# The second MLP products of a two-layer encoder: half of the features by seven block products in place of eight

## The chip, the cores and the metric

The kernel runs on one core of a Trainium2 chip. The metric is the device time of one execution, in microseconds (us). A core has five engines with instruction queues of their own, each worked through in order: TensorE (PE in the profile, its weight loads PEld) multiplies matrices and writes to PSUM, VectorE (DVE) and ScalarE (ACT) do elementwise work on SBUF and PSUM, GpSimd (POOL) elementwise work on SBUF, and SyncE (SP) starts the DMAs from HBM. Semaphores hold an instruction back until what it needs is there.

## The reference

A trunk of two layers on 256 tokens of width 1024, in float32. Each layer has an attention mixer, different in the two layers, and a squared-ReLU MLP with 4096 hidden features. Only the MLP is touched here:

```python
def rms_norm(x, g):
    xf = x.astype(jnp.float32)
    y = xf * lax.rsqrt(jnp.mean(xf * xf, axis=-1, keepdims=True) + RMS_EPS)
    return (y * g.astype(jnp.float32)).astype(x.dtype)

def sq_relu_mlp(xn, w1, w2):
    return jnp.square(jax.nn.relu(xn @ w1)) @ w2

for layer in range(DEPTH):
    ...
    x = x + sq_relu_mlp(rms_norm(x, norm_mlp[layer]), mlp_w1[layer], mlp_w2[layer])
return rms_norm(x, norm_final)
```

The second product is (256 tokens x 4096) times (4096 x 1024) in each layer.

## The kernel before, in words

All weights arrive from HBM in chunks of 128 x 2048 float32 (1 MB). TensorE multiplies in fp32r, a rounded float32, so each operand is split in two: a high half (the value rounded to fp32r, a cast by ScalarE, L227) and a low half (what the rounding left, a subtraction by VectorE, L228). A product a·b is then three matmuls, high·high, high·low, low·high, which `mm3` (L230 to L233) adds up in one PSUM bank. In the up product of the MLP the first two are one matmul of 512 columns, since the high and low halves of x lie side by side (L417), and the third is one of 256 (L420).

The MLP takes 16 blocks of 256 hidden features. For block j, `up(j)` computes the hidden features of all 256 tokens from chunk w1[j] in two PSUM banks; ScalarE copies the part from x's low half to SBUF (`side`, L423), VectorE adds it (`u`, L424) and makes relu(u) times u (`hsq`, L426), and the result is split into `hh` and `hl`. It lies as hidden features x tokens: two blocks of 128 features (f), each with 256 tokens. The second product of block j takes chunk w2[j]: for both f, both blocks of 128 tokens (t) and both halves of the 1024 output features there is one `mm3` with 128 stationary token columns and 512 moving weight columns: 8 `mm3`, 24 matmuls of 512 columns. They add up in four banks, `acc`, over the 16 blocks. The second products run three blocks behind the up products, so a step of the loop holds the second product of j and the up product of j + 3. The last two (first MLP) or three (second MLP) chunks are kept for the end and worked off bank by bank, so that what follows can begin with the first bank.

The order of the work: `weight()` (L218) hands out chunks in the order of `specs`, in which w1 and w2 chunks alternate; on each call it starts the DMA of the chunk four ahead and has the split of the chunks up to two ahead written down. There are four raw buffers and three pairs of split ones, so the split of a chunk waits until PE is done with the one three before it. A scheduler then sets the order of each engine's queue by the order in the program and by priorities, and sets the waits.

GpSimd has next to no work: a few constants, four copies, two memsets and five small powers. `y` (in `hand_over_tokens`) takes the four banks of the first MLP, scaled by each token's inverse norm, to the transposes that make x feature-first again; `finish` adds the second MLP to x, norms it and writes it out.

Of the kernel before, what the change touches and what calls it, by code (L numbers as in the profile page):

```python
# [76 lines left out]
def trunk(ctx, tc, a, out):  # L77
# [29 lines left out]
    def quarter_pair(name):  # L107
        return [act.tile([P, KT // 2, T], F32R, tag="quarter", name=name + v, bufs=4) for v in "hl"]

    def bank(tag):  # L110
        return ps.tile([P, 512], F32, tag=tag, name=tag)

# [31 lines left out]
    specs = []  # L144

    def plan(name, n):
# [25 lines left out]

    parts = {}
# [12 lines left out]

    def split_tiles(j):

        z = [wsp.tile([P, WCH + P], F32R, tag=n, name=n) for n in ("whi", "wlo")]
        return [z[0][:, specs[j][2][0]:specs[j][2][0] + WCH + (LINE if specs[j][3] else 0)], z[1][:, specs[j][2][1]:specs[j][2][1] + WCH]]  # L190

# [8 lines left out]
    def split_piece(eng=None):  # L200
        j, i = divmod(state["split"], WPARTS)
        if i == 0:
            parts[j][1:] = split_tiles(j)
        raw, hi, lo = (z[:, cut(j, i, WPARTS)] for z in parts[j])
        state["split"] += 1
        if specs[j][3] and i == WPARTS - 1:
# [133 lines left out]
    def hand_over_tokens(accs, last, n, scale):  # L340
# [4 lines left out]
        def leave(h, t):  # L345
            last(h, t)
            acc, sc = accs[2 * t + h], column(scale, t)
            with tc.high_priority(NORM_PRIO):
                y = ys[h, t] = scratch([512], "y")
                nc.scalar.activation(y[:, 0:T], acc[:, 0:T], AF.Copy, scale=sc)  # L350
                nc.vector.tensor_scalar(y[:, T:2 * T], acc[:, T:2 * T], sc, None, ALU.mult)
# [47 lines left out]

    def mlp(mp, xT, s, invert, tail, make_down, beside=lambda j: None):  # L400


        hs = {}

        def up(j):
# [3 lines left out]

            pu = [bank("w") for _ in range(2)]  # L410

# [14 lines left out]
            nc.vector.scalar_tensor_tensor(h, u, 0.0, u, ALU.max, ALU.mult)  # L426
# [7 lines left out]
        inv = invert()  # L434
        accs = open_accs()
        down = make_down(accs, hs)
# [7 lines left out]
        return accs, hs, inv, {j: weight() for j in tail}  # L444

# [7 lines left out]
    def mlp_between(mp, xT, s):  # L453
        def down(accs, hs):
            def step(j, w, f):
                for i in range(4):
                    down_tokens(accs[i], hs, j, w, f, i // 2, i % 2 * 512, i % 2 * 512 + 512, (j, f) == (0, 0), False)
            return step

        accs, hs, inv, w = mlp(mp, xT, s, lambda: inverse_columns(s), range(14, 16), down)  # L460

        def last(h, t):
            for j in w:
                for f in range(2):
                    down_tokens(accs[2 * t + h], hs, j, w[j], f, t, h * 512, h * 512 + 512, False, (j, f) == (15, 1))

        return accs, last, inv

    def finish(mp, xT, s):
# [3 lines left out]
        xt = mp.tile([P, NT, D], F32, name="xt")  # L473
        tail = range(13, 16)

        mm = down_tokens

        def down(accs, hs):
            def step(j, w, f):
                for i in range(4):  # L480
                    end = tail[0] - 1 if i == 3 else 15
                    mm(accs[i], hs, j, w, f, i // 2, (i % 2) * 512, (i % 2) * 512 + 512, (j, f) == (0, 0), (j, f) == (end, 1))
            return step

        def tokens_first(j):

            if j % 2 == 0 and j < 8:
                t, h = j // 4, j // 2 % 2
                pt = bank("w")
# [4 lines left out]
        accs, hs, inv, w = mlp(mp, xT, s, lambda: inverse_columns(s), tail, down, tokens_first)  # L494
        jf = [(j, f) for j in w for f in range(2)]
        for j, f in jf:
            for h in range(2):
                mm(accs[h], hs, j, w[j], f, 0, h * 512, h * 512 + 512, False, (j, f) == (15, 1))

# [3 lines left out]
        def square_sum(v, o):  # L503
            nc.scalar.activation(scratch([v.shape[-1]], "junk"), v, AF.Square, scale=D ** -0.5, accum_out=o)

        ss = small.tile([P, 4], F32, tag="ssf", name="ss")
        for h, cs in enumerate(HALF):
# [10 lines left out]
        ss = small.tile([P, 4], F32, tag="ssf", name="ss")  # L518
        xg = mp.tile([P, D], F32, name="xg")
        residual(1, HALF[1], accs[3])  # L520
        for i, (c0, c1) in enumerate(((0, 512), (512, 768), (768, D))):
            acc = bank("w") if i else accs[2]
            for n, (j, f) in enumerate(jf):
# [631 lines left out]
def _layout(i):  # L1155
# [25 lines left out]
    d["w1"] = f(i["mlp_w1"].reshape(2, KT, P, 16, 256).transpose(0, 3, 2, 1, 4).reshape(2, 16, P, WCH))  # L1181
    d["w2"] = f(i["mlp_w2"].reshape(2, 16, 2, P, D).transpose(0, 1, 3, 2, 4).reshape(2, 16, P, WCH))

# [31 lines left out]
```

## Time and profile before

| what | value |
|---|---|
| median of three runs | 736.88 us (736.64 to 737.38) |
| profiled execution, its own time | 737.34 us |
| span of the profile | 735.5 us |
| granted PE clock | 0.998 |
| busy: PE, DVE, ACT, POOL | 727.9, 544.2, 473.5, 8.3 us |
| moved from HBM | 127.16 MB read, 174 GB/s over the span |

The span is the time from the first to the last instruction; what lies around it is 1.84 us here. In a row of a group of instructions stand the line of the program, engine, operation, output and inputs by name with their shapes, the count, then after the bar the time in which any of them ran, the mean duration of one in ns, and the idle time before them with what ended it. In a row of the timeline stand the start, the duration, and the same names. Matmuls overlap in the records: one of 512 columns lasts some 390 ns but the next starts after 227, so a step is counted by starts. The first MLP's products run from 113 to 290 us, the second's from 551 to 729 us.

### The profile page before, as it was taken

The page shows a single profiled execution, that of the slowest core. Times are in us where ns is not written, and L with a number is a line of the kernel's source. Part 1 is how long each engine was busy: PE and PEld are TensorE (multiplying, and loading weights), DVE is VectorE, ACT ScalarE, POOL GpSimd, SP SyncE. Part 2 cuts the span into 40 slices and gives each one's busy share as a digit, 9 for nine tenths or more (in the row PEclk, how much of TensorE's full clock was granted, in tenths as well). Part 3 has the DMA queues.
Part 4 walks back from the last instruction along what each step waited for, and adds up shares of the span by engine and source line. Part 5 has one row for each costly group of instructions (what it writes and reads, how often), then busy time and mean ns, then how long its engine had stood idle before and what let it go on. Part 6 is the DMA issues. An engine that isn't in the chain of part 4 may idle for free.

```text
span 735.5 us, 12087 instructions
## 1 busy us (share of the span) xinstructions
PE 727.9 (99%) x4539; PEld 628.8 (85%) x4539; DVE 544.2 (74%) x1159; ACT 473.5 (64%) x1073; POOL 8.3 (1%) x20
## 2 busy tenths in 40 slices
PE   9999999999999999999999999999999999999996
PEld 7988998888888887888888888888898888888885
DVE  6788859766665666789978886899559765665674
ACT  6788967554455456577877668696857555455441
POOL 0100000000000001000000000000000000000000
PEclk9999999999999999999999999999999999999999
DMA  9873335564555554645664554455545555555501
GB/s 285 323 261 113 115 115 172 179 223 172 194 206 176 204 192 155 230 160 182 206 221 144 191 181 175 147 194 186 178 153 187 214 172 196 203 174 188 211 3 57
DMA packets 24730, 133.17 MB, mean 181 GB/s; under 512 B 3680, under 2 KB 5088, under 8 KB 10336
## 3 DMA queue, kind: packets, MB, share of 16 engines
q1 hardware_dynamic: 24528, 132.28, 52.2%
q8 instruction: 35, 0.57, 0.3%
q14 instruction: 23, 0.19, 0.1%
q10 hardware_dynamic: 144, 0.13, 0.1%
HBM read 127.16 MB, written 1.05 MB: 174 GB/s over the span
## 4 chain that ended last, share of the span: by engine, by line
PE 93%; ACT 2%; DVE 1%; issue 1%; DMA 1%; SPq 0%; POOLq 0%; POOL 0%; DVEq 0%
PE w L417 16%; PE acc L231 13%; PE acc L232 13%; PE acc L233 13%; PE acc L932 10%; PE w L420 8%; PE acc L937 5%; PE acc L584 3%; PE w L1044 1%; PE w L240 1%; PE w L231 1%; PE w L795 1%; PE w L232 1%; PE w L233 1%; PE w L809 1%
## 5 line engine op out<-in xcount | busy, mean ns | idle before, releaser
L228 DVE TENSOR_TENSOR wlo<-raw,whi 128x512 fp32r<-128x512 f32 (+3 forms) x527 | 307.5, 625 | 67.0 <-ACT whi L227 66.1
L227 ACT CAST whi<-raw 128x512 fp32r<-128x512 f32 (+3 forms) x527 | 269.2, 570 | 134.9 <-PE acc L233 57.0
L417 PE MATMUL w<-pair,whi 128*128 128x512 f32 x512 | 122.3, 391 | 0.0
L417 PEld LDWEIGHTS w<-pair,whi 128*128 128x128 f32 x512 | 95.5, 188 | 20.0 <-DVE pair L268 0.5
L231 PE MATMUL acc<-whi,hh 128*128 128x512 f32 x250 | 98.1, 392 | 0.0
L232 PE MATMUL acc<-wlo,hh 128*128 128x512 f32 x250 | 97.8, 391 | 0.0
L233 PE MATMUL acc<-whi,hl 128*128 128x512 f32 x250 | 97.6, 390 | 0.0
L932 PE MATMUL acc<-pair,whi 128*128 128x512 f32 x384 | 96.5, 398 | 0.0
L932 PEld LDWEIGHTS acc<-pair,whi 128*128 128x128 f32 x384 | 69.4, 188 | 13.7 <-issue 0.2
L420 PEld LDWEIGHTS w<-pair,wlo 128*128 128x128 f32 x512 | 63.0, 188 | 2.7
L424 DVE TENSOR_TENSOR u<-w,side 128x256 f32<-128x256 f32 x64 | 27.0, 422 | 51.4 <-ACT side L423 51.3
L420 PE MATMUL w<-pair,wlo 128*128 128x256 f32 x512 | 63.5, 277 | 0.0
L227 ACT CAST hh<-hsq 128x512 fp32r<-128x512 f32 x32 | 19.9, 622 | 56.6 <-DVE hsq L426 56.6
L233 PEld LDWEIGHTS acc<-whi,hl 128*128 128x128 f32 x250 | 47.0, 188 | 9.8
L231 PEld LDWEIGHTS acc<-whi,hh 128*128 128x128 f32 x250 | 47.0, 188 | 8.9
L232 PEld LDWEIGHTS acc<-wlo,hh 128*128 128x128 f32 x250 | 46.9, 188 | 8.8
L937 PEld LDWEIGHTS acc<-pair,wlo 128*128 128x128 f32 x384 | 47.7, 188 | 2.1
L937 PE MATMUL acc<-pair,wlo 128*128 128x256 f32 x384 | 49.0, 278 | 0.0
L231 PE MATMUL acc<-whi,pair 128*128 128x512 f32 x80 | 32.2, 403 | 0.0
L232 PE MATMUL acc<-wlo,pair 128*128 128x512 f32 x80 | 31.3, 391 | 0.0
L233 PE MATMUL acc<-whi,pair 128*128 128x512 f32 x80 | 31.2, 390 | 0.0
L1035 ACT ACTIVATE pp<-sn,dmn 128x384 f32<-128x384 f32 x32 | 19.6, 613 | 9.0 <-DVE dmn L1033 8.2
(221 smaller groups left out, 1103.0 us busy)
## 6 DMA issues: line engine op xcount, KB each, us to landing
raw<-in_w SPq DMA_DIRECT2D x64, 1024.0 KB, 4.8
raw<-in_w_oqk SPq DMA_DIRECT2D x24, 1024.0 KB, 4.9
raw<-in_w_ov SPq DMA_DIRECT2D x12, 1024.0 KB, 4.9
raw<-in_w_qk SPq DMA_DIRECT2D x4, 1024.0 KB, 9.3
raw<-in_w_oe SPq DMA_DIRECT2D x4, 1024.0 KB, 5.2
sw<-qk SPq DMA_DIRECT2D x64, 64.0 KB, 2.0
raw<-in_w_oo SPq DMA_DIRECT2D x4, 1024.0 KB, 5.6
bias<-in_rpb SPq DMA_DIRECT2D x8, 256.0 KB, 3.8
```

The lines of the kernel that those rows point to most:

```text
L227: a = nc.scalar.copy(hi, src).ins
L228: return a, (eng or nc.vector).tensor_tensor(lo, src, hi.bitcast(F32), op=ALU.subtract).ins
L231: nc.tensor.matmul(o, sh, mh, start=first, stop=False)
L232: nc.tensor.matmul(o, sh, ml, start=False, stop=False)
L233: nc.tensor.matmul(o, sl, mh, start=False, stop=last)
L417: nc.tensor.matmul(two(pu[f]), w[0][:, late(cut_of(k, f)) if (k, f) == (KT - 1, 1) else cut_of(k, f)], xT[2][:, k], start=k == 0, stop=False)
L420: nc.tensor.matmul(pu[f][:, 0:T], w[1][:, cut_of(k, f)], xT[0][:, k, :], start=False, stop=k == KT - 1)
L424: nc.vector.tensor_tensor(u[:, f], pu[f][:, 0:T], side[:, f], op=ALU.add)
L584: nc.tensor.matmul(o[:, 0:n], xs[i], (w[1], w[1], w[2])[i], start=(k, i) == (0, 0), stop=(k, i) == (KT - 1, 2))
L932: nc.tensor.matmul(two(hold["p"][f]), hold["w"][0][:, late(c) if f == 1 and k == KT - 1 else c], xp[:, k], start=k == 0, stop=False)
L937: nc.tensor.matmul(hold["p"][f][:, 0:T], hold["w"][1][:, c], xh[:, k, :], start=False, stop=k == KT - 1)
L1035: nc.scalar.activation(pp, sn, AF.Exp, bias=mn, scale=-1.0, accum_out=z)
```

## The change

The second products are done in another way for the first 14 blocks of the first MLP and the first 13 of the second (`SEVEN`).

One half of the output features (512) is computed as before, with two banks (`sums`, one for each token block). For the other half, hidden features x tokens is seen as 2 x 2 blocks of 128 x 128 (f and t), and the weights as 2 x 2 blocks of 128 x 256. A 2 x 2 block product by Strassen's method (in Winograd's form) needs seven products in place of eight. Each is one `mm3` with 256 moving columns, 21 matmuls of 256 columns, which add up over the blocks j in seven half banks (`seven_at`). The method needs four sums of token blocks and four sums of weight blocks for each j. GpSimd makes them: `wsum` (1024 columns, three instructions, written down where the chunk's DMA is) and `hsum` (512 columns, four instructions of 128, after `hsq`). The sums are split like everything else, into `uh`, `ul` and the second half of `whi`, `wlo`; three of the four weight blocks themselves are needed as well and go to `sh`, `sl`. Behind the loop the seven sums are put together to the 2 x 2 result (`second`) by a copy and four additions, and added in `hand_over_tokens` and `finish`.

The banks for this come from the up product: PSUM's second group of four is now `w1` and `w2` with two banks each; from the fourth up product on it has only the two of `w1`. The buffers of `hh` and `hl` go from four to three.

```diff
+SEVEN = (14, 13)
...
     def bank(tag):
-        return ps.tile([P, 512], F32, tag=tag, name=tag)
+
+        if tag == "w":
+            tag, turns[0] = ("w1", "w1", "w2", "w2")[turns[0] % 4], turns[0] + 1
+        return ps.tile([P, 512], F32, tag=tag, name=tag, bufs=4 if tag == "acc" else 2)
...
+            if j - 2 < SEVEN[layer]:
+                seven.add(len(specs))
             specs.append((a["w2"][layer, j - 2], WCH, (0, 0), False))
...
         parts[j] = [raw, None, None]
+        if j in seven:
+
+            r, v = raw[:, 1024:WCH], state["mp"].tile([P, 1024], F32, tag="wsum", name="wsum", bufs=3)
+            nc.gpsimd.tensor_tensor(v[:, 0:512], r[:, 256:768], r[:, 0:512], op=ALU.subtract)
+            nc.gpsimd.tensor_tensor(v[:, 512:768], r[:, 512:768], v[:, 0:256], op=ALU.subtract)
+            nc.gpsimd.tensor_tensor(v[:, 768:1024], v[:, 512:768], r[:, 768:1024], op=ALU.subtract)
+            sums[j] = v
...
         state["split"] += 1
+        if j in seven:
+            raw, *z = parts[j]
+            for y, c, src in (((z[0:2], (0, 1024), raw[:, 0:1024]),), (), ((z[4:6], (0, T), raw[:, 1024:1280]), (z[4:6], (T, 3 * T), raw[:, 1536:WCH])),
+                              ((z[2:4], (0, 1024), sums[j]),))[i]:
+                split(*(v[:, slice(*c)] for v in y), src, eng)
+            return
...
-            hs[j] = tuple(mp.tile([P, 512], F32R, tag=n, name=n, bufs=4) for n in ("hh", "hl"))
+            hs[j] = tuple(mp.tile([P, 512], F32R, tag=n, name=n, bufs=3) for n in ("hh", "hl"))
             split(*hs[j], h)
+            if j < tail[0]:
+
+                q, v = [h[:, tok(i)] for i in range(4)], mp.tile([P, 4, P], F32, tag="hsum", name="hsum", bufs=2)
+                for o, x0, x1, op in ((0, q[1], q[3], ALU.add), (1, q[0], q[1], ALU.subtract), (2, q[3], v[:, 1], ALU.subtract),
+                                      (3, q[2], v[:, 2], ALU.subtract)):
+                    nc.gpsimd.tensor_tensor(v[:, o], x0, x1, op=op)
+                hs[j] += tuple(mp.tile([P, 512], F32R, tag=n, name=n, bufs=3) for n in ("uh", "ul"))
+                split(*hs[j][2:], v.rearrange("p a b -> p (a b)"))
...
         for j in range(tail[0]):
             w = weight()
+            for b, half, (of, at), c in products:
+                o, l, m = seven_at[b][:, half * T:half * T + T], [z[:, tok(at)] for z in hs[j][2 * of:2 * of + 2]], [z[:, c % 4 * T:c % 4 * T + T] for z in w[2 + c // 4 * 2:][:2]]
+                mm3(o, *l, *m, j == 0 and half == 0, j == tail[0] - 1 and (half == 1 or b == 3))
             for f in range(2):
-                down(j, w, f)
+                for t in range(NT):
+                    down_tokens(sums[t], hs, j, w, f, t, f * -512, f * -512 + 512, (j, f) == (0, 0), False)
+            beside(j)
             if j + 3 < 16:
                 up(j + 3)
-            beside(j)
...
+        z, g = scratch([2, T], "z"), mp.tile([P, 4, T], F32, name="second")
+        nc.scalar.copy(z, two(seven_at[2]))
+        side = lambda v: v.unsqueeze(1).broadcast_to([P, 2, T])
+        nc.vector.tensor_tensor(g[:, 0:4:3], two(seven_at[0]), side(z[:, 0]), op=ALU.add)
+        nc.vector.tensor_tensor(g[:, 1:3], two(seven_at[1]), side(g[:, 3]), op=ALU.add)
+        nc.vector.tensor_tensor(g[:, 1:4:2], g[:, 1:3], side(z[:, 1]), op=ALU.add)
+        nc.vector.tensor_tensor(g[:, 2], g[:, 2], seven_at[3][:, 0:T], op=ALU.subtract)
```

GpSimd's queue in the first MLP. Before, between the last copy of the first mixer and the first memset of the second:

```order
L742 COPY ktok<-kpe 128x4x32 [waits DVE_49,PE_49]
L871 MEMSET k_0_3291 128x1024 [waits DVE_49,PE_49]
```

With the change, one step of the loop and the start of the next stand there (`raw` is a weight chunk, `wsum` and `hsum` the sums):

```order
L199 TENSOR_TENSOR wsum<-raw 128x512 [waits DMAHW7_49,Activation_49]
L200 TENSOR_TENSOR wsum<-raw,wsum 128x256 [waits Pool_49]
L201 TENSOR_TENSOR wsum<-wsum,raw 128x256 [waits Pool_49]
L474 TENSOR_TENSOR hsum<-hsq 128x128 [waits DVE_49,Activation_49]
L474 TENSOR_TENSOR hsum<-hsq 128x128
L474 TENSOR_TENSOR hsum<-hsq,hsum 128x128 [waits Pool_49] x2
L199 TENSOR_TENSOR wsum<-raw 128x512 [waits DMAHW1_49,Activation_49]
```

Seven instructions of 1536 columns a step are new, and the sums of a step's tokens stand ahead of those of a later chunk's weights.

VectorE's queue for one step in the middle of the first MLP, before (`whi`, `wlo` are the halves of a weight chunk, `w` a bank of the up product):

```order
L228 TENSOR_TENSOR wlo<-raw,whi 128x512 [waits DMAHW4_49,Activation_49]
L228 TENSOR_TENSOR wlo<-raw,whi 128x512 [waits Activation_49] x2
L228 TENSOR_TENSOR wlo<-raw,whi 128x384 [waits Activation_49]
L228 TENSOR_TENSOR wlo<-raw,whi 128x128 [waits Activation_49]
L424 TENSOR_TENSOR u<-w,side 128x256 [waits Activation_49]
L228 TENSOR_TENSOR wlo<-raw,whi 128x512 [waits DMAHW5_49,PE_49]
L228 TENSOR_TENSOR wlo<-raw,whi 128x512
L424 TENSOR_TENSOR u<-w,side 128x256 [waits Activation_49]
L228 TENSOR_TENSOR wlo<-raw,whi 128x512
L426 SCALAR_TENSOR_TENSOR hsq<-u 128x512 [waits DVE_49]
L228 TENSOR_TENSOR wlo<-raw,whi 128x512
L228 TENSOR_TENSOR hl<-hsq,hh 128x512 [waits Activation_49]
```

and with the change:

```order
L259 TENSOR_TENSOR wlo<-raw,whi 128x512 [waits DMAHW6_49,Activation_49]
L259 TENSOR_TENSOR wlo<-raw,whi 128x512 [waits Activation_49] x2
L259 TENSOR_TENSOR wlo<-raw,whi 128x384 [waits Activation_49]
L259 TENSOR_TENSOR wlo<-raw,whi 128x128 [waits Activation_49]
L259 TENSOR_TENSOR wlo<-raw,whi 128x1024 [waits PE_49,Activation_49]
L464 TENSOR_TENSOR u<-w_3051,side 128x256 [waits Activation_49]
L464 TENSOR_TENSOR u<-w_3052,side 128x256 [waits Activation_49]
L259 TENSOR_TENSOR wlo<-wsum,whi 128x1024
L466 SCALAR_TENSOR_TENSOR hsq<-u 128x512 [waits DVE_49]
L259 TENSOR_TENSOR sl<-raw,sh 128x256 [waits DMAHW1_49,PE_49,Activation_49]
L259 TENSOR_TENSOR sl<-raw,sh 128x512 [waits Activation_49]
L259 TENSOR_TENSOR hl<-hsq,hh 128x512 [waits Activation_49]
L259 TENSOR_TENSOR ul<-hsum,uh 128x512 [waits Activation_49]
```

The w2 chunk, four pieces of 512 columns before, is now 1024 raw, 1024 sums, 256 and 512 raw. Both additions `u` stand behind the first of these and together, where before two pieces lay between them, and `ul` is new behind `hl`.

ScalarE's queue of the same step with the change, from the casts of the w2 chunk on:

```order
L258 CAST whi<-raw 128x1024 [waits PE_49,Activation_49]
L258 CAST whi<-wsum 128x1024
L463 COPY side<-w_2451 128x256 [waits PE_49]
L463 COPY side<-w_2452 128x256 [waits PE_49]
L258 CAST sh<-raw 128x256 [waits DMAHW7_49,PE_49]
L258 CAST sh<-raw 128x512
L258 CAST hh<-hsq 128x512 [waits DVE_49]
L258 CAST uh<-hsum 128x512 [waits Pool_49]
L258 CAST whi<-raw 128x512 [waits DMAHW6_49,PE_49,Activation_49]
```

The cast `uh` waits for GpSimd, and the next w1 chunk's casts stand behind it.

More of the change, by code (lines that the diff above doesn't have):

```diff
@@ L144, in trunk @@
     specs = []
+    seven = set()
     def plan(name, n):
@@ L406, in up @@
             w = weight()
-            pu = [bank("w") for _ in range(2)]
+            pu = [bank("w" if j < 3 else "w1") for _ in range(2)]
             ranges = [range(4), range(4, 6), range(6, 8)] if j == 0 else [range(8)]
@@ L453, in mlp_between @@
     def mlp_between(mp, xT, s):
[L454 to L460, printed above, removed]
+        hs, inv, w, sums, second = mlp(mp, xT, s, lambda: inverse_columns(s), range(SEVEN[0], 16))
+        for t in range(NT):
+            nc.scalar.activation(second[t], second[t], AF.Copy, scale=column(inv, t))
+        accs = {}
         def last(h, t):
+            acc = accs[2 * t + h] = bank("acc") if h else sums[t]
             for j in w:
                 for f in range(2):
-                    down_tokens(accs[2 * t + h], hs, j, w[j], f, t, h * 512, h * 512 + 512, False, (j, f) == (15, 1))
-        return accs, last, inv
+                    down_tokens(acc, hs, j, w[j], f, t, h * 512, h * 512 + 512, h == 1 and (j, f) == (SEVEN[0], 0), (j, f) == (15, 1))
+        return accs, last, (inv, second)
     def finish(mp, xT, s):
@@ L473, in finish @@
         xt = mp.tile([P, NT, D], F32, name="xt")
-        tail = range(13, 16)
+        tail = range(SEVEN[1], 16)
         mm = down_tokens
[L478 to L483, printed above, removed]
         def tokens_first(j):
@@ L504, in square_sum @@
             nc.scalar.activation(scratch([v.shape[-1]], "junk"), v, AF.Square, scale=D ** -0.5, accum_out=o)
+        for t in range(NT):
+            residual(t, HALF[1], second[t])
         ss = small.tile([P, 4], F32, tag="ssf", name="ss")
@@ L518, in finish @@
         ss = small.tile([P, 4], F32, tag="ssf", name="ss")
-        xg = mp.tile([P, D], F32, name="xg")
-        residual(1, HALF[1], accs[3])
+        xg = second[2]
         for i, (c0, c1) in enumerate(((0, 512), (512, 768), (768, D))):
-            acc = bank("w") if i else accs[2]
+            acc = bank("w1") if i else sums[1]
             for n, (j, f) in enumerate(jf):
```

45 lines of the change are left out of this document (32 added, 13 removed).

## The prediction, made before the changed kernel ran

> **What bounds the kernel now.** I read the page's shares first, then the chain of waits, then the second products' steps, engine by engine.
>
> ```profile
> span 735.5 us, 12087 instructions
> PE 727.9 (99%) x4539; PEld 628.8 (85%) x4539; DVE 544.2 (74%) x1159; ACT 473.5 (64%) x1073; POOL 8.3 (1%) x20
> ...
> PE 93%; ACT 2%; DVE 1%; issue 1%; DMA 1%; SPq 0%; POOLq 0%; POOL 0%; DVEq 0%
> ```
>
> TensorE (PE) is 93% of the chain that ends last, so work taken from PE shortens the span until something else ends later. GpSimd (POOL) is nearly unused. Inside the first MLP the chain in order of time repeats itself:
>
> ```profile
> 146.91 3.63 PE w L417 x16
> 150.54 1.82 PE w L420 x16
> 152.36 0.23 PE acc L231
> ...
> 157.83 3.63 PE w L417 x16
> ...
> 168.75 3.63 PE w L417 x16
> ```
>
> One step is one block of 256 hidden features: an up product and a second product. It takes 157.83 - 146.91 = 10.92 us, and so does the next. The 16 matmuls of 512 columns at L417 take 3.63 us (0.227 each), the 16 of 256 columns at L420 1.82 us (0.114 each), which leaves 5.47 us for the 24 second products of 512 columns (0.228 each). A matmul of 256 columns thus costs half of one of 512 although it loads its own weights. VectorE (DVE) in the same step:
>
> ```profile
> 147.64 2.57 DVE L228 TENSOR_TENSOR wlo<-raw,whi 128x512 fp32r<-128x512 f32 x5 [1.50 <-ACT whi L227]
> 152.02 0.43 DVE L424 TENSOR_TENSOR u<-w,side 128x256 f32<-128x256 f32 x1 [1.81 <-ACT side L423]
> 152.40 1.29 DVE L228 TENSOR_TENSOR wlo<-raw,whi 128x512 fp32r<-128x512 f32 x2
> 153.61 0.42 DVE L424 TENSOR_TENSOR u<-w,side 128x256 f32<-128x256 f32 x1
> ...
> 154.54 0.69 DVE L426 SCALAR_TENSOR_TENSOR hsq<-u 128x512 f32<-128x512 f32 x1
> ...
> 155.92 0.69 DVE L228 TENSOR_TENSOR hl<-hsq,hh 128x512 fp32r<-128x512 f32 x1
> 158.56 2.57 DVE L228 TENSOR_TENSOR wlo<-raw,whi 128x512 fp32r<-128x512 f32 x5 [1.95 <-ACT whi L227]
> ```
>
> VectorE works in three bursts and waits between them. Ten steps together:
>
> ```profile
> 147.00:257.00 110.00, 110.00 (x565) 93.98 (x564) 70.84 (x131) 57.04 (x122) 0.00 (x0) 1.00 0.57 195
> ```
>
> The columns after the length are PE, PEld, DVE, ACT, POOL busy, granted clock, DMA share and GB/s. VectorE is busy 70.84 / 110 x 10.92 = 7.03 us of a step, ScalarE 5.66, GpSimd nothing.
>
> **What leaves PE.** In a step with the change, 12 of the 24 matmuls of 512 columns stay, and 12 become 21 of 256 columns (seven products, three matmuls each). 12 x 0.228 = 2.74 us leave and 21 x 0.114 = 2.39 come: PE's own step is 10.92 - 0.345 = 10.575 us. There are 14 such steps in the first MLP and 13 in the second, so the most that can be gained is 27 x 0.345 = 9.3 us. The DMA bytes stay as they are.
>
> **What comes to the other engines, per step.** The price of one more column comes from these rows of ten steps:
>
> ```profile
> L228 DVE TENSOR_TENSOR wlo<-raw,whi 128x512 fp32r<-128x512 f32 x71 | 46.3, 687 | 21.0 <-ACT whi L227 21.0
> L424 DVE TENSOR_TENSOR u<-w,side 128x256 f32<-128x256 f32 x20 | 8.4, 422 | 18.1 <-ACT side L423 18.1
> L228 DVE TENSOR_TENSOR wlo<-raw,whi 128x128 fp32r<-128x128 f32 x10 | 2.9, 285 | 0.0
> L227 ACT CAST whi<-raw 128x512 fp32r<-128x512 f32 x72 | 40.7, 620 | 34.9 <-PE acc L233 21.8 <-PE w L417 13.1
> L227 ACT CAST whi<-raw 128x128 fp32r<-128x128 f32 x10 | 2.9, 295 | 0.0
> ```
>
> VectorE: (687 - 285) / 384 = 1.05 ns a column. The w2 chunk is split in 1024 + 256 + 512 + 1024 = 2816 columns in place of 2048, and the token sums add 512: 1280 columns, 1.34 us, and one instruction more, about 0.1 (of the 0.15 us that 285 ns holds beyond its columns, part overlaps the one before). So 7.03 becomes 8.5 us. ScalarE: (620 - 295) / 384 = 0.85 ns, 1280 columns and a start, 1.2 us: 5.66 becomes 6.9. Both fit in 10.575 if nothing else holds them.
>
> GpSimd: seven TENSOR_TENSORs, 512 + 256 + 256 columns for weights and four times 128 for tokens, 1536 columns. No such instruction is in the trace. The nearest rows are these:
>
> ```profile
> L742 POOL COPY ktok<-kpe 128x128 f32<-128x128 f32 x4 | 1.2, 294 | 33.8 <-DVE qk_l L228 25.1 <-PE acc L809 8.7
> L137 POOL MEMSET mhalf<- 128x1 f32 x1 | 0.1, 98 | 0.0
> ```
>
> (294 - 98) / 128 = 1.53 ns a column with one input. If a second input is free, seven starts of 0.098 and 1536 columns make 0.69 + 2.35 = 3.0 us. If it is read after the first, 0.69 + 4.70 = 5.4 us. I take the middle, 4.2. The Trainium skill (GPSIMD Engine Reference, section 3.1) has 4497 ns for an fp32 tensor_tensor add of 2048 columns, 2.2 ns a column, which as an estimate would give 4.1 us; no run here shows it yet.
>
> **Whether GpSimd works beside VectorE** decides the case, and the trace has two small answers. The same instruction, a power on 128x2 or 128x1, alone and beside a VectorE instruction whose two inputs both lie in SBUF:
>
> ```profile
> 25.70 0.71 POOL L293 TENSOR_TENSOR rstd<-ms,mhalf 128x2 f32<-128x2 f32 x1 [24.26 <-DVE ms L287]
> ...
> 31.91 0.68 DVE L228 TENSOR_TENSOR wlo<-raw,whi 128x512 fp32r<-128x512 f32 x1
> 32.08 1.06 POOL L596 TENSOR_TENSOR rstd<-ss,mhalf 128x2 f32<-128x2 f32 x1 [3.54 <-DVE ss L594]
> ...
> 49.83 0.29 POOL L742 COPY ktok<-kpe 128x128 f32<-128x128 f32 x1 [16.69 <-DVE qk_l L228]
> 49.89 0.41 DVE L780 CUSTOM_DVE_ANT_0 sn<-w,bias 128x256 f32<-128x256 f32 x1
> ...
> 722.99 0.55 POOL L258 TENSOR_TENSOR rstd<-ss,mhalf 128x1 f32<-128x1 f32 x1 [408.68 <-DVE ss L510]
> ...
> 730.48 0.42 DVE L533 TENSOR_TENSOR xg<-xt,gain 128x256 f32<-128x256 f32 x1
> 730.64 0.67 POOL L258 TENSOR_TENSOR rstd<-ss,mhalf 128x1 f32<-128x1 f32 x1 [7.10 <-DVE ss L531]
> ```
>
> Alone 0.71, beside the split 1.06; alone 0.55, beside xg 0.67. The split ends at 31.91 + 0.68 = 32.59 and the power 0.55 us later, at 33.14; xg ends at 730.90 and the power 0.41 later, at 731.31. If GpSimd waits about 0.15 us into its instruction for VectorE to end, the first loses 0.36 and the second 0.11, and 0.35 and 0.12 are seen. The copy at 49.83 ran beside a VectorE instruction that has one of its inputs in PSUM (sn from w) and took the usual 0.29. So I read: a GpSimd instruction that reads SBUF and a VectorE instruction with two SBUF inputs take turns. The trace shows only GpSimd waiting; that VectorE waits in its turn I assume.
>
> The Trainium skill says so in SBUF — State Buffer, section "Who interferes with whom": such a pair contends for one read interface, and whoever comes second waits for the other's whole instruction. The two rows agree in the one direction; by this rule VectorE would wait too, and the sum is the one below, and without it the sum is the second rival's.
>
> Of VectorE's 8.5 us the two additions u (2 x 0.42, one input in PSUM) are free of this, which leaves 7.6 us that must alternate with GpSimd's 4.2: 11.8 us, more than the 10.575 of PE and than the 10.92 of today. If the starts of GpSimd's instructions (0.69) lie beside VectorE's work, it is 11.1. I take 11.5, between them.
>
> The order makes the turns hurt: on VectorE the low half ul of the token sums stands directly behind hl, and it waits for ScalarE's uh, which waits for four GpSimd instructions that can start only after hsq. Behind uh on ScalarE stand the five casts of the next w1 chunk, behind ul on VectorE their low halves, and PE waits for those two chunks later. Meanwhile GpSimd goes on with the next 512 weight columns, and ul waits for it.
>
> **The sum.** The profiled execution took 737.34 us (span 735.5 and 1.84 around it), 0.46 over the median of 736.88. Steps with a w1 chunk beside the products: 13 in each MLP. The split runs up to one chunk ahead, so I let the first step of each MLP go at PE's pace, as well as the last of the first MLP, which has no up product left: 3 x -0.345 = -1.0. The other 24 cost 11.5 - 10.92 = 0.58 each, 13.9. Behind each loop stand one copy (0.62, as the cast of 512) and four additions on VectorE (three of 0.69, one of 0.42), 3.1 us, under the last products of sums: 24 x 0.228 = 5.5 us in the first MLP, 18 x 0.228 = 4.1 in the second, before a bank of the seven is wanted again. Covered, I take 0.35 for each; uncovered it would be 3.1 each, 6 in all. 737.3 - 1.0 + 13.9 + 0.7 = **751 us**, about 2% slower.
>
> **The rivals.**
>
> PE stays the bound, because the two engines don't really take turns, or the sums are cheap: with 3.0 us for GpSimd, 7.6 + 3.0 = 10.6 is PE's own step. For it: GpSimd's rows show a wait of at most 0.35 us, the trace never shows VectorE waiting, and without turns VectorE has 10.575 - 8.5 = 2.1 us left. Against it: both pairs of rows agree to 0.01 us with waiting till the end. Then 737.3 - 9.3 + 0.7 = 729 us, up to 735 with part of the waits.
>
> GpSimd is at its upper bound: 7.6 + 5.4 = 13.0 us a step, 24 x 2.1 = 50, about 787 us. For it: one input costs 1.53 ns already. Against it: 294 ns at 128 columns may hold a fixed part of reading that longer instructions don't repeat.
>
> Two banks in place of four. The up product now writes to two banks that the next one needs again, so PE waits until both u additions are done. Today the second ends at 153.61 + 0.42 = 154.03, 1.67 us after the up product's end (152.36), and the next up product starts at 157.83; with the change 5.13 us lie between. The additions now stand behind the 1024 columns of raw weights (1.2 us), and their copies on ScalarE behind two casts of 1024 columns (1.0 each): from the point where u is over 3.4 us later than today, each further us costs 24 x 1 us. One us over gives 737.3 - 9.3 + 24 + 0.7 = 753 us, without any taking of turns.
>
> That the change doesn't do what it says, that is, that 21 matmuls cost more than 12 of double length, is against L420's 0.114 and gets no chance of its own.
>
> **How the numbers follow.** Turns with a step over 10.95: 0.53. PE the bound: 0.31. GpSimd at its upper bound: 0.05. Two banks: 0.05. A step between, where loss and gain cancel: 0.06. A difference within 0.2% (1.5 us) can't be told from none here. Faster 0.31, same 0.06, slower 0.63. The likeliest case by itself runs from 739 (step 11.0) to 767 (step 12.2). The range takes in the second case but for its very end, and leaves out the upper bound of GpSimd: 728 to 772.
>
> **What would show it.** Rows of GpSimd's TENSOR_TENSORs: under 1 us for 512 columns speaks for the second case, 1.7 for the third. VectorE's mean of 687 ns for a split of 512 columns: it must grow if VectorE waits for GpSimd. The chain: products with steps of 10.6 us if PE is the bound, else ScalarE, VectorE and GpSimd in it with some 15 to 20 us more of idle PE. The prediction is wrong if GpSimd's rows and VectorE's 687 ns stay unstretched side by side, or if PE's step is not 10.575 where nothing waits.

## The result, and the profile after

The changed kernel takes 787.44 us (median of four runs, 785.04 to 787.88) against 737.04 before: 1.0675 times the time, interval 1.0662 to 1.0687. It is slower, as forecast, but by 50 us where 14 were forecast, and lies outside the stated range.

From the page of the changed kernel, its shares and its chain of waits:

```profile
span 786.1 us, 12931 instructions
PE 737.7 (94%) x4782; PEld 640.5 (81%) x4782; DVE 646.8 (82%) x1197; ACT 504.9 (64%) x1102; POOL 181.5 (23%) x209
...
PE 58%; DVE 19%; POOL 10%; issue 8%; ACT 4%; DMA 1%; SPq 0%; POOLq 0%; DVEq 0%
DVE wlo L259 13%; PE acc L988 11%; POOL hsum L474 9%; PE acc L262 6%; PE acc L263 6%; PE acc L264 6%; PE acc L993 6%; PE w L457 6%; PE w L460 2%; PE acc L640 2%; DVE hsq L466 2%; DVE u L464 2%; PE w L262 2%; ACT uh L258 2%; PE w L264 2%
```

PE fell from 93% to 58% of the chain. What took its place are VectorE's low halves, GpSimd's token sums and `issue`, time in which an engine waits for nothing that the profile shows.

Two up products of the changed kernel in the timeline, one step apart (the second row ends at the edge of the window, before its sixteenth matmul):

```profile
191.89 3.95 PE L457 MATMUL w<-pair,whi 128*128 128x512 f32 x16 [1.53 <-DVE u L464]
...
204.41 1.89 PE L457 MATMUL w<-pair,whi 128*128 128x512 f32 x7 [1.52 <-DVE u L464]
```

A step is 12.52 us, 10.92 before, and PE idles 1.5 us in each, waiting for VectorE's `u`. So go seven steps in the middle of the first MLP; the mean of all 24 is 11.99. Five of the seven, from 191.89 to 254.52, VectorE's groups by shape (busy, mean ns of one, idle before):

```profile
L259 DVE TENSOR_TENSOR wlo<-raw,whi 128x512 fp32r<-128x512 f32 x15 | 16.1, 1126 | 0.0
L259 DVE TENSOR_TENSOR wlo<-raw,whi 128x384 fp32r<-128x384 f32 x5 | 4.9, 986 | 0.0
L259 DVE TENSOR_TENSOR sl<-raw,sh 128x512 fp32r<-128x512 f32 x5 | 4.7, 948 | 0.0
L259 DVE TENSOR_TENSOR hl<-hsq,hh 128x512 fp32r<-128x512 f32 x5 | 4.7, 946 | 0.0
L464 DVE TENSOR_TENSOR u<-w,side 128x256 f32<-128x256 f32 x11 | 4.1, 409 | 0.0
L259 DVE TENSOR_TENSOR wlo<-raw,whi 128x128 fp32r<-128x128 f32 x5 | 3.6, 715 | 0.0
L259 DVE TENSOR_TENSOR ul<-hsum,uh 128x512 fp32r<-128x512 f32 x5 | 3.5, 693 | 7.7 <-ACT uh L258 7.7
```

A split of 512 columns took 687 ns before and takes 1126 here; `u`, which has one input in PSUM, is not stretched (422 before, 409 here). Together VectorE's instructions lose 3 x 0.44 + 0.43 + 0.26 + 0.26 + 0.43 = 2.7 us a step. The last row holds the other loss: `ul` waits 7.7 / 5 = 1.54 us a step for `uh`. VectorE is busy 10.98 us of a step:

```profile
191.89:254.52 62.63, 54.99 (x326) 47.36 (x326) 54.90 (x71) 33.40 (x65) 31.94 (x35) 1.00 0.45 169
```

Its own work is thus 10.98 - 2.7 = 8.3 us, and 8.3 + 2.7 + 1.54 = 12.5: in these steps VectorE's queue fills the whole step. The chain inside a step shows what stands behind the wait (start, duration, what):

```profile
180.70 0.69 DVE hsq L466
...
181.52 1.39 POOL hsum L474 x2
182.91 0.07 issue
182.98 0.80 POOL hsum L474
183.78 0.07 issue
183.84 0.47 POOL hsum L474
...
184.34 0.63 ACT uh L258
...
184.99 0.04 DVE ul L259
```

GpSimd's four token sums take from 181.52 to 184.31, 2.8 us, where its shortest instructions of 128 columns take 0.45 each: the second and third, 0.91 and 0.79, ran beside `sl` and `hl`.

Where the 50.6 us of the two spans went, by the starts of the up products in the two timelines (us):

| stretch | before | after | difference |
|---|---|---|---|
| first MLP, first to fourth up product | 22.9 | 33.6 | +10.7 |
| first MLP, the twelve steps after it | 130.7 | 143.8 | +13.1 |
| second MLP, first to fourth up product | 23.3 | 38.4 | +15.1 |
| second MLP, the twelve steps after it | 132.6 | 144.1 | +11.5 |
| all the rest | | | +0.2 |

Half of the loss lies ahead of the fourth up product; in what follows that stretch is called the start of an MLP. What PE waited for, summed over the changed kernel (us in total, times, longest):

```profile
PE w L457 <- DVE u L464: 15.7, 11, 2.0
PE w L457 <- ACT xt L546: 9.5, 3, 4.1
PE w L262 <- DVE u L464: 9.3, 2, 4.8
PE w L316 <- DVE squares L309: 3.8, 1, 3.8
```

The second row is in the second MLP alone: the transposes of x beside the products take a bank of `w1`, ScalarE's copy out of it (`xt`) stands behind `uh`, and the up product waits for the bank. There only one step takes 12.52 us; the three with this wait take 16.73, 15.74 and 13.55, most others 10.7 to 11.6. The third row is the start of each MLP, where the first banks of the second products wait for the `u` of the third up product. In the first MLP that `u` stands behind a `ul` that waits for `uh`:

```profile
136.66 0.69 DVE L259 TENSOR_TENSOR ul<-hsum,uh 128x512 fp32r<-128x512 f32 x1 [1.53 <-ACT uh L258]
137.27 0.42 DVE L464 TENSOR_TENSOR u<-w,side 128x256 f32<-128x256 f32 x1
...
137.74 0.80 PE L262 MATMUL w<-whi,hh 128*128 128x512 f32 x1 [4.53 <-DVE u L464]
```

The matmuls at the long waits also ran at a lower granted clock (the number behind the busy times):

```profile
137.70:141.00 3.30, 3.26 (x8) 2.61 (x9) 3.30 (x6) 2.33 (x6) 1.48 (x2) 0.50 0.30 72
639.50:642.70 3.20, 3.20 (x8) 2.53 (x9) 2.97 (x4) 1.47 (x4) 2.64 (x2) 0.50 0.00 0
```

In the two MLPs of the change there are six such stretches, five of 3.4 us and one of 6.8, each at a wait of PE of 2.5 to 4.8 us; the waits of 1.5 us show none, and in the kernel before the clock is 1.00 throughout both MLPs. PE was busy in at least 21 of these 24 us, with matmuls of 512 columns starting 0.43 us apart (138.76, 139.19, 139.61) where 0.23 is usual. At the full clock the same work would take about half as long, so some 10 of the 50 us, an estimate and an upper bound, go to the clock as a consequence of the waits. No run tests this by itself.

### The profile page after: what moved, and what is told of

The parts are those of the page before. It is cut to its first block, busy times and chain, and to the rows that moved or that the text cites. A ratio compares the mean times of both kernels' runs of the same rounds, so it can differ in the third digit from the quotient of the medians.

```text
span 786.1 us, 12931 instructions
## 1 busy us (share of the span) xinstructions
PE 737.7 (94%) x4782; PEld 640.5 (81%) x4782; DVE 646.8 (82%) x1197; ACT 504.9 (64%) x1102; POOL 181.5 (23%) x209
## 4 chain that ended last, share of the span: by engine, by line
PE 58%; DVE 19%; POOL 10%; issue 8%; ACT 4%; DMA 1%; SPq 0%; POOLq 0%; DVEq 0%
DVE wlo L259 13%; PE acc L988 11%; POOL hsum L474 9%; PE acc L262 6%; PE acc L263 6%; PE acc L264 6%; PE acc L993 6%; PE w L457 6%; PE w L460 2%; PE acc L640 2%; DVE hsq L466 2%; DVE u L464 2%; PE w L262 2%; ACT uh L258 2%; PE w L264 2%
## 5 line engine op out<-in xcount | busy, mean ns | idle before, releaser
L259 DVE TENSOR_TENSOR wlo<-raw,whi 128x512 fp32r<-128x512 f32 (+4 forms) x446 | 313.8, 747 | 30.4 <-ACT whi L258 20.4
L258 ACT CAST whi<-raw 128x512 fp32r<-128x512 f32 (+4 forms) x446 | 234.2, 586 | 63.8 <-issue 20.1
L199 POOL TENSOR_TENSOR wsum<-raw 128x512 f32<-128x512 f32 x27 | 40.6, 1503 | 325.8 <-DVE wlo L259 225.9
L474 POOL TENSOR_TENSOR hsum<-hsq 128x128 f32<-128x128 f32 x54 | 44.3, 839 | 112.9 <-DVE hsq L466 109.4
L262 PE MATMUL w<-whi,hh 128*128 128x512 f32 (+1 forms) x140 | 55.6, 397 | 9.3 <-DVE u L464 9.3
L264 PE MATMUL w<-whi,hl 128*128 128x512 f32 (+1 forms) x140 | 55.0, 393 | 0.0
L263 PE MATMUL w<-wlo,hh 128*128 128x512 f32 (+1 forms) x140 | 54.9, 392 | 0.0
L259 DVE TENSOR_TENSOR sl<-raw,sh 128x256 fp32r<-128x256 f32 (+1 forms) x54 | 33.0, 650 | 0.0
L474 POOL TENSOR_TENSOR hsum<-hsq,hsum 128x128 f32<-128x128 f32 x54 | 31.9, 590 | 4.1
L259 DVE TENSOR_TENSOR wlo<-wsum,whi 128x1024 fp32r<-128x1024 f32 x27 | 32.7, 1211 | 0.0
```

Of the source, the lines that this page charges most:

```text
L199: nc.gpsimd.tensor_tensor(v[:, 0:512], r[:, 256:768], r[:, 0:512], op=ALU.subtract)
L258: a = nc.scalar.copy(hi, src).ins
L259: return a, (eng or nc.vector).tensor_tensor(lo, src, hi.bitcast(F32), op=ALU.subtract).ins
L262: nc.tensor.matmul(o, sh, mh, start=first, stop=False)
L263: nc.tensor.matmul(o, sh, ml, start=False, stop=False)
L264: nc.tensor.matmul(o, sl, mh, start=False, stop=last)
```

## The experiments

The theory after the first profile: **turns**. GpSimd and VectorE wait for each other at SBUF, in both directions, and what VectorE loses adds to its waits in its own queue. The rivals: the **work and its order** (more splits, `u` later, two banks in place of four) would be slow without GpSimd, too; and the **chain of waits** through GpSimd would be slow whatever GpSimd does there. Times in the table are medians of three rounds and a profiled run where an interval stands, else single runs; starts and steps are worked out from the starts of the up products.

| kernel | time, us | against before | first to fourth up product, 1st and 2nd MLP | mean of the 12 steps, 1st and 2nd MLP |
|---|---|---|---|---|
| before | 737.0 | 1 | 22.9, 23.3 | 10.89, 11.05 |
| the change | 787.44 | 1.0675 | 33.6, 38.4 | 11.98, 12.00 |
| no sums | 731.59 | 0.9922 (0.9906 to 0.9939) | 24.7, 26.0 | 10.50, 10.59 |
| memsets for sums | 731.24 | 0.9918 (0.9903 to 0.9933) | 24.9, 26.2 | 10.48, 10.56 |
| all sums by VectorE | 732.65 | 0.9939 (0.9924 to 0.9953) | 24.0, 24.4 | 10.63, 10.75 |
| before, sums beside it | 773.40 | single | 36.3, 37.8 | 11.09, 11.25 |
| weight sums only | 742.30 | single | 28.6, 30.1 | 10.63, 10.59 |
| token sums only | 755.09 | single | 31.4, 34.2 | 10.63, 11.21 |
| token sums by VectorE | 742.06 | single | 27.1, 29.2 | 10.69, 10.81 |
| first sums by VectorE | 776.66 | single | 25.6, 26.5 | 12.44, 12.30 |
| split one step later | 781.05 | single | 32.0, 36.3 | 11.90, 11.86 |
| token sums unread | 748.96 | single | 30.8, 33.0 | 10.73, 10.73 |

**No sums.** The weights' sums become one constant tile, the token sums `hsq` itself; every split stays.

```diff
-            r, v = raw[:, 1024:WCH], state["mp"].tile([P, 1024], F32, tag="wsum", name="wsum", bufs=3)
-            nc.gpsimd.tensor_tensor(v[:, 0:512], r[:, 256:768], r[:, 0:512], op=ALU.subtract)
...
-            sums[j] = v
+            sums[j] = state["fixed"]
...
-                split(*hs[j][2:], v.rearrange("p a b -> p (a b)"))
+                split(*hs[j][2:], h)
```

> The changed kernel without GpSimd's sums: the seven products stay, all splits keep their sizes and their order in the middle of the loop, but they split a constant tile (weights) and hsq itself (tokens), so the result is not the reference's. Theory of turns (GpSimd and VectorE wait for each other at SBUF): VectorE's split of 512 columns is back at 687 ns, the step at PE's 10.6 us, the time at 728 to 738 us. Rival (the longer queues do it: more splits, additions u late, two banks in place of four): the split is back at 687 ns too, but the step stays above 11.5 us and the time above 760 us.

Measured: 731.59 us, the regular step 10.69, the split of 512 columns 689 ns. The rival of work and order falls: with all splits, with `u` late and with two banks, the kernel is 0.8% faster than before. Two up products in its chain, one step apart:

```profile
168.27 3.63 PE w L455 x16
...
178.96 3.63 PE w L455 x16
```

Two things I had not expected: the step is 10.69 and not 10.575, and the start of each MLP is still 2 to 3 us longer than before, though the step right behind it makes up for that (8.36 and 8.00 us, where 10.57 and 11.07 were taken before).

**Memsets for sums.** GpSimd's seven instructions write the same tiles and read nothing; all waits stay.

```diff
-            nc.gpsimd.tensor_tensor(v[:, 0:512], r[:, 256:768], r[:, 0:512], op=ALU.subtract)
...
+            for c in ((0, 512), (512, 768), (768, 1024)):
+                nc.gpsimd.memset(v[:, c[0]:c[1]], 0.5)
...
-                    nc.gpsimd.tensor_tensor(v[:, o], x0, x1, op=op)
+                    nc.gpsimd.memset(v[:, o], 0.5)
```

> The seven sums of a step are memsets of the same tiles and columns, so GpSimd writes SBUF but reads nothing, and every wait between the engines stays; the result is not the reference's. If the turns are about reading SBUF: splits at 687 ns, the four 128-column instructions take 0.8 us in place of 2.7 us, step 10.6 to 10.9 us, 729 to 742 us. If writing counts as well: splits of 512 columns at 750 ns or more while a memset runs. If the chain of waits hsq, GpSimd, uh, ul is the cause, whatever GpSimd does: step above 11.3 us, over 750 us.

Measured: 731.24 us. In its timeline a split of 512 columns and `hl` beside GpSimd's memsets:

```profile
198.31 1.04 POOL L200 MEMSET wsum<- 128x512 f32 x3 [8.90 <-ACT uh L257]
198.71 0.68 DVE L258 TENSOR_TENSOR ul<-hsum,uh 128x512 fp32r<-128x512 f32 x1
...
199.46 0.65 POOL L473 MEMSET hsum<- 128x128 f32 x4
199.65 0.69 DVE L258 TENSOR_TENSOR hl<-hsq,hh 128x512 fp32r<-128x512 f32 x1
```

0.68 and 0.69 us, unstretched: what GpSimd writes costs VectorE nothing here, so the turns are about reading. The chain of waits as such isn't tested by it, since it is short here (four memsets in 0.65 us).

**All sums by VectorE.** The whole computation, with `nc.vector` for `nc.gpsimd` in the seven lines of sums.

```diff
-                    nc.gpsimd.tensor_tensor(v[:, o], x0, x1, op=op)
+                    nc.vector.tensor_tensor(v[:, o], x0, x1, op=op)
```

> All sums by VectorE in place of GpSimd, nothing left out. VectorE has some 8.5 + 1.6 + 0.5 = 10.6 us of work in a step, as much as PE. Theory of turns: no stretched splits, step 10.7 to 11.5 us, 733 to 755 us, faster than with GpSimd although VectorE has more to do. Rival (VectorE's work and its queue's order are the bound, GpSimd's help is worth its while): slower than the 787 us of the change, step above 12.6 us.

Measured: 732.65 us, 0.6% faster than before and 55 us faster than the change, although VectorE has no pause left in a stretch of regular steps (third busy time of the row, 67.00 of 67.00):

```profile
190.00:257.00 67.00, 67.00 (x405) 59.63 (x404) 67.00 (x137) 44.22 (x84) 0.00 (x0) 1.00 0.62 219
```

This version beats both kernels.

**Before, sums beside it.** The kernel before, with seven GpSimd instructions for each block on a tile that nobody else touches.

```diff
             split(*hs[j], h)
+            for n in (512, 256, 256, 128, 128, 128, 128):
+                nc.gpsimd.tensor_tensor(load[2][:, 0:n], load[0][:, 0:n], load[1][:, 0:n], op=ALU.subtract)
```

> The kernel before, with the same seven GpSimd instructions a step (512, 256, 256 and four of 128 columns) on a tile of their own that nobody else reads. Theory of turns: VectorE's split of 512 columns grows from 687 ns to some 900 ns while GpSimd works, GpSimd's 512 columns take 1.2 us alone and up to 1.8 us beside VectorE; VectorE has idle time for it, so the time grows by less than 10 us. Rival (no turns): 687 ns and one fixed duration for GpSimd's 512 columns, the time within 2 us of before.

Measured: 773.4 us, 36 more, where I expected less than 10. My edit was not what I had in mind: as these instructions wait for nothing, GpSimd ran all 112 of an MLP one after the other from its first up product on. So it shows a different thing: a GpSimd load that nobody waits for costs this kernel 28 us at the two starts (36.3 - 22.9 and 37.8 - 23.3), the lower clock behind PE's waits of 7.6 us included (0.50 for some 10 us at each). In two regular steps with GpSimd still at work (163.9 to 185.8) VectorE's split of 512 columns took 1004 ns in the mean and the step stayed 10.92: turns alone cost nothing where VectorE's queue still fits into PE's step. In its timeline, `u` beside GpSimd's 128 columns is untouched, and so is GpSimd (0.47 us, shortest 0.45):

```profile
170.18 0.41 DVE L427 TENSOR_TENSOR u<-w,side 128x256 f32<-128x256 f32 x1
170.19 0.47 POOL L433 TENSOR_TENSOR load<-load 128x128 f32<-128x128 f32 x1
```

**Weight sums only, token sums only.** Each leaves out the other's GpSimd instructions as in the kernel without sums.

> The changed kernel with GpSimd's weight sums (512, 256 and 256 columns a step) and without its token sums: uh and ul split hsq itself, so the result is not the reference's. Theory of turns, each instruction of one engine behind one of the other: VectorE's 8.4 us of a step and GpSimd's 2.8 us (1.27, 0.75 and 0.75 as its shortest instructions took) make 11.2 us at the most, and the wait of VectorE for uh (1.55 us a step) is gone: step 10.7 to 11.2 us, 732 to 748 us. Rival (the weight sums are what costs, the token sums are small and hidden): over 765 us.

> The changed kernel with GpSimd's token sums (four instructions of 128 columns a step) and without its weight sums: the second half of whi and wlo splits a constant tile, so the result is not the reference's. Theory of turns: VectorE's 8.4 us, what it loses to GpSimd's 1.8 us, and the wait for uh of 1.55 us: step 10.7 to 11.7 us, 732 to 760 us, and the start of each MLP, where three blocks' token sums come one after the other, keeps a part of its loss. Rival (the weight sums are what costs): the time of the kernel without any sums, 732 us.

Measured: 742.3 and 755.1 us. In both the regular steps of the first MLP are back at PE's 10.69 us: VectorE's queue with either kind alone still fits, with the token sums even though the wait for `uh` stays. Only both together exceed PE's step. The token sums are the dearer half, by the starts (31.4 and 34.2 us) and by the second MLP's steps, where PE still waits 4.9 us for `xt`. The rival in both expectations falls, as neither half is small.

**Token sums by VectorE**, weight sums by GpSimd, nothing left out.

> Token sums by VectorE, weight sums by GpSimd, nothing left out. Theory of turns: VectorE has 8.4 + 0.9 us, GpSimd 2.8 us that alternate with all but the 0.8 us of u, and uh waits for VectorE's own instructions only: step 11.2 to 12.1 us, 745 to 770 us, slower than all sums by VectorE (732.65) although VectorE does less. Rival (VectorE's load is the bound): faster than 732.65 us.

Measured: 742.06 us, a little below what I expected, since the steps are PE's. It is slower than all sums by VectorE, though VectorE does less: the starts are 8 us longer. What I did not expect is GpSimd's 512 columns, here from 190 to 257 us and in one step:

```profile
L199 POOL TENSOR_TENSOR wsum<-raw 128x512 f32<-128x512 f32 x7 | 31.0, 4424 | 22.7 <-DMA raw<-in_w 22.7
...
210.22 4.30 POOL L199 TENSOR_TENSOR wsum<-raw 128x512 f32<-128x512 f32 x1 [3.37 <-DMA raw<-in_w]
210.87 0.68 DVE L259 TENSOR_TENSOR ul<-hsum,uh 128x512 fp32r<-128x512 f32 x1
211.47 1.88 DVE L259 TENSOR_TENSOR wlo<-raw,whi 128x384 fp32r<-128x384 f32 x3
...
213.28 0.74 DVE L464 TENSOR_TENSOR u<-w,side 128x256 f32<-128x256 f32 x2
```

They took 4.42 us in the mean in place of 1.27, while VectorE's instructions with two SBUF inputs followed each other unstretched (`ul` 0.68). In all ten such steps of the first MLP GpSimd's sum ended 1.22 to 1.24 us after VectorE's next `u` began (here 214.52 and 213.28), about its own 1.27: it got in with the first instruction that has an input in PSUM.

**First sums by VectorE.** The token sums of three blocks and the weight sums of two chunks of each MLP move to VectorE, the rest stays with GpSimd.

```diff
-            nc.gpsimd.tensor_tensor(v[:, 0:512], r[:, 256:768], r[:, 0:512], op=ALU.subtract)
+            (nc.vector if len(sums) % SEVEN[0] < 2 else nc.gpsimd).tensor_tensor(v[:, 0:512], r[:, 256:768], r[:, 0:512], op=ALU.subtract)
...
-                    nc.gpsimd.tensor_tensor(v[:, o], x0, x1, op=op)
+                    (nc.vector if j < 3 else nc.gpsimd).tensor_tensor(v[:, o], x0, x1, op=op)
```

> The changed kernel, but the token sums of the first three blocks and the weight sums of the first two chunks of each MLP by VectorE; the rest by GpSimd as in the change. If the 10.7 and 15.1 us that the change loses between the first and the fourth up product come from GpSimd's sums being bunched there, they fall to 0 to 3 us, while the later steps stay at 12.5 us: 787 - 20 = 767 us, give or take 6. If the loss there only moves on to the next steps, the time stays above 777 us.

Measured: 776.66 us, between the two. The starts fall by 20 us (33.6 to 25.6, 38.4 to 26.5), so it is GpSimd's bunched sums that made them long; but the twelve steps behind grow by 9 (12 x 0.46 + 12 x 0.30). Probably the late start had let some of the later sums be made during its waits, and that is given back; no run shows this by itself.

**Split one step later.** `uh` and `ul` of a block were written down in the next up product. The scheduler put them back behind the sums of their own block, with the same wait, so the run tells nothing of what it was made for; its 781.05 us go with the unchanged step of 12.52.

```diff
-                split(*hs[j][2:], v.rearrange("p a b -> p (a b)"))
+                    split(*hs[j][2:], v.rearrange("p a b -> p (a b)"))
+                pending.append(later)
```

> The changed kernel with uh and ul of a block split one step later, at the same place in ScalarE's and VectorE's queues, so that both find GpSimd's token sums long done; nothing left out. In the change a step is 12.53 us: VectorE's own 8.4, 2.7 lost in turns, 1.55 of waiting for uh. If these add up in VectorE's queue, 1.55 leaves: step 10.7 to 11.2 us, and the time falls by 24 x 1.4 = 33 us to 745 to 760 us (the losses at the start of each MLP stay). If the turns alone set the step (7.6 us of VectorE with two SBUF inputs and 4.66 us of GpSimd by its shortest instructions, 12.3 us), what is saved by not waiting is lost to more turns: step 12.0 to 12.6 us, 775 to 788 us.

**Token sums unread.** GpSimd makes all sums, but `uh` and `ul` split `hsq` at the same place, so the wait for GpSimd is gone and the turns stay.

```diff
-                split(*hs[j][2:], v.rearrange("p a b -> p (a b)"))
+                split(*hs[j][2:], h)
```

> The changed kernel with all of GpSimd's sums made as in the change, but uh and ul split hsq itself at the same place in the queues: nobody reads the token sums, and ScalarE and VectorE no longer wait for them; the result is not the reference's. (The split one step later did not take the wait away: the scheduler put uh back behind the sums of its own block.) If VectorE's own 8.4 us, the turns (2.7) and the wait for uh (1.55) add up to the step of 12.53: step 10.7 to 11.2 us, 745 to 760 us. If the turns alone set the step (7.6 and 4.66 us, 12.3): step 12.0 to 12.6 us, 775 to 788 us, with more lost in turns.

Measured: 748.96 us, the regular step 10.69 for most of the first MLP and up to 11.45 in its last steps. The forecast from the sum of both losses holds, that from the turns alone falls. `ul` now is in the turns, as the steps from 190 to 257 us show:

```profile
L259 DVE TENSOR_TENSOR wlo<-raw,whi 128x512 fp32r<-128x512 f32 x20 | 16.7, 884 | 0.0
L259 DVE TENSOR_TENSOR ul<-hsq,uh 128x512 fp32r<-128x512 f32 x6 | 5.7, 948 | 0.0
L259 DVE TENSOR_TENSOR sl<-raw,sh 128x512 fp32r<-128x512 f32 x6 | 5.7, 948 | 0.0
```

Without the wait 787.4 - 749.0 = 38 us are gone, and the turns, with nothing waiting for the token sums, still cost 749.0 - 731.6 = 17 us, 13 of them at the starts. Both differences include what the clock does (0.50 for 6.8 us at each start of this run, nowhere in the MLPs of the kernel without sums). They are not two prices that add up: without the weight sums the wait stays and 32 us are gone, since in the regular steps VectorE's queue costs time only as far as it exceeds PE's 10.69 us.

## Why the prediction was right or wrong

**Right: the direction and its cause.** Turns at SBUF, with VectorE waiting too. The prediction only assumed the second half; here are VectorE and GpSimd in the change:

```profile
211.27 1.84 POOL L199 TENSOR_TENSOR wsum<-raw 128x512 f32<-128x512 f32 x1 [1.91 <-DMA raw<-in_w]
211.87 1.79 DVE L259 TENSOR_TENSOR wlo<-raw,whi 128x512 fp32r<-128x512 f32 x1
213.19 1.07 POOL L200 TENSOR_TENSOR wsum<-raw,wsum 128x256 f32<-128x256 f32 x1
```

The split took 1.10 us longer than its own 0.69, and ended 0.55 us after GpSimd's first sum (213.66 and 213.11), about what its 512 columns take. The Trainium skill (SBUF — State Buffer, "Who interferes with whom") has it that the second comer waits for the first one's whole instruction. The trace agrees but for the last 0.14 us: with its own 0.69 us at the end, the split went on at 212.97, where GpSimd's instruction ended at 213.11. The added time, 1.10 us behind 512 columns and 0.26 behind 128 (948 - 687 ns), is less than the 1.27 and 0.45 us of those instructions by themselves, as VectorE came when GpSimd's was under way.

**Where the 37 us lie.** The sum forecast 751 us for the profiled execution, and 787.9 were measured. By the table of stretches, 26.5 of these 37 us lie in the starts (forecast -0.7, measured +25.8) and 10.7 in the 24 steps behind them (forecast +13.9, measured +24.6). Two terms failed, the start more than the step.

**Wrong: "I take 11.5, between them".** The step is 12.5 us in the middle of the first MLP and 11.99 in the mean of the 24. The work was priced well: VectorE's own 8.5 us are 8.3; GpSimd's 4.2 are 4.7 by its shortest instructions (1.27 + 2 x 0.79 + 4 x 0.45), between the two bounds of 3.0 and 5.4. The turns took 2.7 us, while the prediction's 11.5 held 11.5 - 8.5 = 3.0 of them. What it lacked is the wait of `ul` for `uh`, 1.54 us a step. The prediction named this wait in the queue, and even that GpSimd goes on with weights meanwhile, but gave it no time: it counted the turns as if VectorE's queue never stood still. Without the wait the step was 10.7 to 11.4 (token sums unread), with it 12.5. In the second MLP the loss came by another way, the wait for `xt` behind `uh`.

**Wrong: "I let the first step of each MLP go at PE's pace".** The starts were to gain, and lost 25.8 us, a little more than all the steps behind them. Three up products stand there one behind the other, each with token sums, beside two chunks' weight sums and the squares. No regular product lies between to hide them, and PE waited 4.5 and 4.8 us for the `u` that frees the banks of the first second products, then went on at half the clock for a while. With the first sums on VectorE 20 of the 25.8 us went away there, and some 11 us net, so the bunched sums are the cause. Without the wait for `uh` the starts still lose 17.6 of the 25.8 us (token sums unread); what the turns and the clock have in these was not taken apart.

**The rivals.** "PE stays the bound" came true where nothing reads beside VectorE: 731 us, within what was given for it. The third, GpSimd at its upper bound, gave 787 us, which is the measured time by luck: GpSimd wasn't at 5.4 us. Its sign, 1.7 us for 512 columns, can be seen in the five steps,

```profile
L199 POOL TENSOR_TENSOR wsum<-raw 128x512 f32<-128x512 f32 x5 | 8.6, 1719 | 8.9 <-DMA raw<-in_w 8.9
```

but that is the duration with turns; the shortest of the 27 took 1.27 us. "Two banks in place of four" had no price of its own in the first MLP: without sums the same two banks cost nothing. In the second MLP it had one that I did not see, the transposes' bank behind `xt` behind `uh`, 9.5 us in three waits.

**The gain on PE.** The step is 10.69, 0.115 more than 10.575. Consecutive products of 256 columns in the change:

```profile
185.07 0.28 PE L263 MATMUL acc<-sl,hh 128*128 128x256 f32 x1
185.19 0.28 PE L264 MATMUL acc<-sh,hl 128*128 128x256 f32 x1
...
185.66 0.28 PE L262 MATMUL acc<-sh,hh 128*128 128x256 f32 x1
```

Five starts in 0.59 us, 0.118 each and not 0.114; 21 of them make 0.09 us more. The forecast of 9.3 us at the most, 8.6 with the additions behind the loops, is 5.6 measured (no sums): 27 steps of 0.115 us make 3.1, which is all that lacks. The longer starts add nothing, as the step behind each makes up for it. The order of VectorE, ScalarE and GpSimd in the queues was as shown; the additions behind the loops were covered, as forecast (0.2 us for all the rest).

## What to carry to other kernels

An idle GpSimd is not a free engine: where it read SBUF here while VectorE ran instructions with two SBUF inputs, each waited for the other (0.69 us became 1.79 behind 512 columns), and moving the same sums to a VectorE that was busy already was 55 us faster. Price such a change by VectorE's whole queue, its own work plus what it loses in turns plus every wait of an instruction in it, and look at the start of a loop, where no steady work hides bunched extra instructions. A wait that is named in a prediction needs a time of its own.

## What had not been expected of the hardware

GpSimd's reading stretches VectorE by some 2.2 ns a column (1.10 us behind 512 columns, 0.26 behind 128). GpSimd itself takes 0.45 us for 128 and 1.27 us for 512 columns, that is, 2.1 ns a column and 0.18 us beside.

Who goes first is not settled. In the change GpSimd's sums mostly got in behind one VectorE instruction (1.72 us for 512 columns in the five steps). With the token sums on VectorE the same sum waited through a row of unstretched VectorE instructions until `u` (4.42 us in the mean). Why it is the one here and the other there was not tried.
